# Token halves of the MLP made the halves of the output projection: the first half turned between its last products, four first products over 512 tokens among the second half's norms

## The chip, the cores and the metric

The kernel runs on one core of one Trainium2 chip. The metric is the device time of one execution in microseconds (us), the median over several runs; lower is better. The engines are named as the profile names them: PE (TensorE matmuls), PEld (TensorE weight loads), DVE (VectorE), ACT (ScalarE), POOL (GpSimd) and SP (SyncE, which issues most DMAs).

## What is computed

One residual block over 1024 tokens of 1024 channels in float32: two parallel mixers on a normalised input, a gated merge, then the part that the change touches, an output projection, a second RMS norm, an MLP with a squared ReLU, and a final norm. Cut to that part, the reference is:

```python
h = x.astype(jnp.float32) + merged @ w_out[layer].astype(f32)

hn = rmsnorm(h, norm2_g[layer])
a = jnp.square(jax.nn.relu(hn @ w_ff1[layer].astype(f32)))
h = h + a @ w_ff2[layer].astype(f32)
...
return rmsnorm(h, final_g).astype(x.dtype)
```

with SEQ = 1024, D_MODEL = 1024 and D_FF = 4096, and `rmsnorm(x, g)` = x · rsqrt(mean(x²) + 1e-6) · g for each token.

## The kernel before, in words

**Precision.** Each float32 operand of a large product is split into a high part (a cast to fp32r on ACT, line 142, tiles that end in `h`) and a low part (the difference, a subtraction on DVE, line 147, tiles that end in `l`). A product of two split operands is three matmuls: high by high, high by low, low by high (`three`, line 490, recorded by line 121). A product of this stage has four steps of 128 in its contraction, so it is 12 matmuls of 128x512.

**Seven products in place of eight.** The output projection and both MLP products are done by a scheme of the Strassen-Winograd kind: each matrix is cut into two by two blocks, and seven products of sums of blocks replace eight. For the first MLP product the token side is cut into two halves (q = 0 and 1) and the channels into two. The class `Quads` (line 282) holds the token side. `raw[q, kp]` (tiles `hnq`) are the turned norms, channels on the partitions: kp 0 and 1 are the first half of the channels, kp 2 and 3 the second, two blocks of 128 channels to a tile. `hl[i, kp]` (tiles `sqh`, `sql`) are the split operands of product i. Products 1 and 2 use the raw first token half; 6, 5, 7 and 3 use sums of blocks (`sums`, line 341; tiles `sq1` and `hnq` again), and 4 uses a raw block of the second token half.

**The stage.** The stage of the change goes from the last products of the output projection to the first of the MLP (lines 2036 to 2104):

- The output projection ends with `pwV` products for token blocks 4 to 7 (`out_rest`, four of them) and `pwZ` products for the same blocks (`out_last`). A token block is 128 tokens. Its residual rows are in `hres[tb]` (tile `h`); blocks 0 to 3 are one half of the projection's tokens, 4 to 7 the other. Each `pwV` and `pwZ` product is added to `hres[4]` to `hres[7]` by DVE (line 1072). Blocks 0 to 3 are final before the `pwV` products begin; block 4+n is final only after the n-th `pwZ` product.
- Each finished block is normalised (`norm2_token`, line 1443): ACT squares it with a sum (line 1451; block 7 in two pieces, added on POOL by line 1458), POOL scales and takes the power -0.5 (lines 230 and 233), DVE multiplies (line 1462, tile `hn`), and POOL issues the DMA that stores the block (line 1467).
- The norms are turned (`Quads.fill`, line 304): 16 transposes of 128x128 on PE (line 124, into banks `hnt`), four to a bank, then ACT copies the bank to `hnq` (line 329). The first token half is split at once.
- In this kernel the MLP's token halves are the even and the odd token blocks. So every pair of blocks, one even, one odd, gives 128 tokens to each half: the first pair (0, 1) is turned as soon as it is normalised, and the half-done operands let products 1 and 2 of the first two column blocks (`w1`, `w2`; bank `pW`) run over 256 tokens at a time (matmuls of 128x256) as the pairs come in.
- Then come products 6 (`x6`, bank `pX`), 5 (`y5`, bank `pY`), 7, 4 and 3 of the two column blocks, and after them the loop over the other column blocks (`mlp_up`). Product 6 needs the sums of both token halves, and the sums of weights `t1h`, `t1l`.

**What sets the order.** Each engine runs its instructions in the order in which the program gives them to it. The order is that of the calls in the main part, changed by a scheduler under ordering hints: `after(...)` puts one instruction behind another on an engine without a semaphore; ACT copies and squares are chained by `last_evac`; the `sums` and `sum_lo` of DVE are put behind the last low part (`last_lo`). PE is strictly in order within the "fill" lane, where all products of this stage are.

**The end of the kernel.** The second MLP product lands its seven products in `hres` (`land`, line 1901), and `finish_tokens` (line 1809) takes the final norm of each block: the even blocks in the last group's first four steps, the odd ones at the very end.

Of the kernel before, what the change touches and what calls it, by code (L numbers as in the profile page):

```python
# [14 lines left out]
ALU = mybir.AluOpType  # L15
# [4 lines left out]
P = 128  # L20
T = 1024
D = 1024
NT = T // P
KT = D // P
# [15 lines left out]
def kernel(  # L40
# [19 lines left out]
    nc = tc.nc  # L60
# [14 lines left out]
    def slot(name, dt=F32):  # L75
        return spool.tile([P, 1024], dt, tag="s", name=name)
# [216 lines left out]
    class Quads:  # L293
# [7 lines left out]
        def part(t, pr, n):  # L301
            return t.rearrange("p (k t) -> p k t", k=2)[:, :, pr * P : (pr + n) * P]

        def fill(self, pr, src, name):


            banks = []
            for kp in range(KT // 2):
                if pr == 0:
                    for q in range(2):  # L310
                        self.raw[q, kp] = slot(f"{name}q{q}{kp}")
                pb = bank(f"{name}t{pr}{kp}")
                open_block("fill")
                for q in range(2):
# [12 lines left out]
        def leave(self, pr, q, kp, pb):  # L327
            last_evac[0] = after(
                nc.scalar.copy(
                    self.part(self.raw[q, kp], pr, 1),  # L330
                    pb[:, q * 256 : (q + 1) * 256].rearrange("p (k t) -> p k t", k=2),
                ),
                last_evac[0],
            )
# [7 lines left out]
        def sums(self, pr, n, first=True, then=True):  # L342
            r = self.raw

            def tt(out, a, b, op):
                after(
                    nc.vector.tensor_tensor(
                        out=self.part(out, pr, n),
                        in0=self.part(a, pr, n),
                        in1=self.part(b, pr, n),  # L350
                        op=op,
                    ),
                    self.last_lo,
                )

            for kp in range(2):
                if pr == 0 and first:
                    self.s1.append(slot(f"sq1{kp}"))
                if first:
                    tt(self.s1[kp], r[1, kp], r[1, kp + 2], ALU.add)  # L360
                    tt(r[1, kp], r[0, kp], r[1, kp], ALU.subtract)
                    tt(r[0, kp], self.s1[kp], r[0, kp], ALU.subtract)
            for kp in range(2):
                if then:
                    tt(r[0, kp + 2], r[0, kp + 2], r[0, kp], ALU.subtract)

        def sum_form(self, i):
# [8 lines left out]
            for kp in range(2):  # L376
                self.split(i, kp, src[kp])

        def form(self, i, k, c0=0, n=512):
            h, l = self.hl[i, k // 2]  # L380
            c = (k % 2) * 512 + c0
            return h[:, c : c + n], l[:, c : c + n]


    class Unit:
# [1205 lines left out]
    class UpPair:  # L1591
# [63 lines left out]
            self.sum_hi(i)  # L1655
            self.sum_lo(i)

        def product(self, i, ps, start, stop=False, c0=0, n=512, ks=range(4)):
            open_block("fill")
            wh, wl = self.w[i]  # L1660
            for k in ks:
                xh, xl = hn.form(i, k, c0, n)
                three(
                    ps[:, c0 : c0 + n], wh[:, k], wl[:, k], xh, xl, start and k == 0, k == 3, True
                )

        def put(self, m, t, n=1):
            dst = ad[self.j // 2][:, m - 1 : m - 1 + n, self.j % 2, :]
# [2 lines left out]

        def w1(self, c0=0, n=512):
            if c0 == 0:
                self.W = bank(f"pW{self.j}")
                self.p1 = half(f"p1_{self.j}")
            self.product(1, self.W, True, False, c0, n)
            last_evac[0] = nc.scalar.copy(self.p1[:, c0 : c0 + n], self.W[:, c0 : c0 + n])

        def w2(self, c0=0, n=512, ks=range(4)):
            self.product(2, self.W, False, True, c0, n, ks)
            if c0 + n == 512:
                self.a11 = half(f"a11_{self.j}")
                relu_square(self.a11, self.W)
                self.put(3, self.a11)

        def x6(self):
            self.X = bank(f"pX{self.j}")
# [210 lines left out]

    def land(m, tb):
        for q, sign in LANDS[m]:
            h = hres[2 * tb + int(q[0]) - 1]
            cs = slice((int(q[1]) - 1) * 512, int(q[1]) * 512)
            ins = (add if sign > 0 else sub)(h[:, cs], h[:, cs], pmb[m, tb])
        return ins

    def mlp_down():
        for i, (gi, c) in enumerate(steps):
# [5 lines left out]
            if not last or c < NCH - 2:  # L1915
                for o in ops[i]:
                    for tb in range(4):
                        down_products(c, tb, *o)
                        if c == NCH - 1:
                            land(o[0], tb)  # L1920
            else:
                for tb in range(4):
                    for b in (1, 0):
                        down_products(c - b, tb, *ops[i - b][0])
                    landed = land(6, tb)
                    half_ssq(2 * tb + 1, 1)
                    if tb:
                        finish_tokens(2 * tb - 1, landed)
                finish_tokens(NT - 1)
            if i < NT - 1:  # L1930
                for tb in (0, 1) if i == 0 else (i + 1,):
# [3 lines left out]
                gfb[0] = slot("gf")  # L1935
                load(gfb[0], final_g.partition_broadcast(P))
            if last and c < 4:
                half_ssq(2 * c, 0)
                half_ssq(2 * c, 1)
                finish_tokens(2 * c)  # L1940
                half_ssq(2 * c + 1, 0)
                mul(hres[2 * c + 1][:, 0:512], hres[2 * c + 1][:, 0:512], gfb[0][:, 0:512])


    for tb in (0, 1):
# [146 lines left out]
    first[0].sum_split(0)  # L2092
    hn.sum_form(5)
    first[1].sum_hi(0)
    after(first[1].sum_lo(0), hn.last_lo)
    for u in first:
        u.y5()
    hn.sum_form(7)
    for u in first:
        u.x7()  # L2100
    hn.sums(2, 2, first=False)
    hn.sum_form(4)
    pairs[2].split()
    pairs[2].sums()
# [38 lines left out]
```

## Time and profile before

| what | value |
|---|---|
| median of 3 runs | 1470.97 us (1469.83 to 1471.96) |
| span of the profiled execution | 1469.2 us, 20065 instructions |
| busy in the span: PE, PEld | 1441.4 us (98%), 1227.8 us (84%) |
| busy in the span: DVE, ACT, POOL | 1105.7 us (75%), 671.9 us (46%), 132.0 us (9%) |
| mean granted TensorE clock | 0.993 |
| the stage of the change | about 809 to 863 us of the span |

The span goes from the first to the last instruction of one profiled execution; no time of that execution apart from its span is given, and the median of the unprofiled runs lies 1.8 us above the span. Rows of the timeline show the start, the duration, the engine, the line of the code, the operation, output<-inputs and their shape, the number of merged instructions, and in square brackets how long the engine was idle before and who ended that. Matmuls overlap, so the distance between two starts, not the duration, is what one costs. A wait on PE is only lost time if nothing else could be on PE, and as PE is in order, it always is.

### The profile page before, as it was taken

The numbers are of one execution on the slowest core, as the hardware profiler recorded it, in microseconds if no ns is written. First come the engines' busy times: TensorE is split into PE (matmuls) and PEld (weight loads), VectorE is DVE, ScalarE is ACT, GpSimd is POOL, SyncE is SP. The second block draws the span as 40 slices with busy tenths as digits, with TensorE's granted clock in tenths as the row PEclk, the third lists the DMA queues.
The fourth block names the chain that finished last, engine by engine and source line by source line (L and its number), as shares of the span: only waits on it lengthen the run. The fifth ranks groups of instructions, "written<-read, shape, count | busy, mean of one in ns | idle before, by whom it ended". The sixth has DMA issues, their size and how long they took to land.

```text
span 1469.2 us, 20065 instructions
## 1 busy us (share of the span) xinstructions
PE 1441.4 (98%) x7490; PEld 1227.8 (84%) x7490; DVE 1105.7 (75%) x1591; ACT 671.9 (46%) x1180; POOL 132.0 (9%) x319
## 2 busy tenths in 40 slices
PE   8999998999999999999999899999999999999997
PEld 8889987988898888888888688888888888888886
DVE  6699797789657788877777888666766666768765
ACT  7566665552313234532344465444444533533433
POOL 3121111000000002100010300000000000000032
PEclk9999999999999999999999999999999999999999
DMA  7144255001313148665589223444444975676834
GB/s 206 35 119 101 46 106 110 27 15 44 93 30 100 51 129 234 227 208 179 170 270 302 101 79 123 158 158 158 157 157 158 345 272 201 231 276 246 281 104 179
DMA packets 157736, 227.30 MB, mean 155 GB/s; under 512 B 25308, under 2 KB 92936, under 8 KB 157640
## 3 DMA queue, kind: packets, MB, share of 16 engines
q1 hardware_dynamic: 142664, 184.07, 37.3%
q0 software_dynamic: 11376, 35.40, 9.3%
q10 hardware_dynamic: 3600, 6.56, 1.2%
q8 instruction: 59, 0.97, 0.3%
q14 instruction: 37, 0.30, 0.1%
HBM read 163.34 MB, written 62.65 MB: 154 GB/s over the span
## 4 chain that ended last, share of the span: by engine, by line
PE 89%; DVE 5%; DMA 2%; POOL 1%; issue 1%; ACT 1%; SPq 0%; POOLq 0%; ACTq 0%; DVEq 0%
PE pm L121 18%; PE pX L121 9%; PE pjqk L121 6%; PE pY L121 6%; PE pW L121 6%; PE pjv L121 3%; PE pys L121 3%; PE gY L121 3%; PE gX L121 3%; PE pyh L121 3%; PE pji L121 3%; PE pjg L121 3%; PE pjf L121 3%; PE po L121 3%; PE pjq L121 2%; PE z L121 2%
## 5 line engine op out<-in xcount | busy, mean ns | idle before, releaser
L142 ACT CAST whid<-w 128x1024 fp32r<-128x1024 f32 x31 | 32.6, 1052 | 154.1 <-PE pm L121 86.2
L679 DVE TENSOR_TENSOR_SCAN rm<-rm,bits 128x511 f32<-128x511 f32 (+7 forms) x72 | 87.3, 1219 | 15.2 <-ACT rm L657 13.5
L121 PE MATMUL pm<-wlod,sh 128*128 128x512 f32 x248 | 96.7, 390 | 0.7 <-DVE wlod L147 0.7
L121 PE MATMUL pm<-whid,sl 128*128 128x512 f32 x248 | 96.6, 390 | 0.0
L121 PE MATMUL pm<-whid,sh 128*128 128x512 f32 x248 | 96.6, 389 | 0.0
L147 DVE TENSOR_TENSOR wlod<-w,whid 128x1024 fp32r<-128x1024 f32 x31 | 37.9, 1223 | 57.2 <-ACT whid L142 57.2
L121 PE MATMUL pm<-th,sh 128*128 128x512 f32 x200 | 77.9, 390 | 0.0
L121 PE MATMUL pm<-th,sl 128*128 128x512 f32 x200 | 77.9, 389 | 0.0
L121 PE MATMUL pm<-tl,sh 128*128 128x512 f32 x200 | 77.9, 389 | 0.0
L147 DVE TENSOR_TENSOR sl<-sa,sh 128x1024 fp32r<-128x1024 f32 x56 | 68.3, 1219 | 0.8 <-ACT sh L142 0.8
L142 ACT CAST wTh<-pw 128x512 fp32r<-128x512 f32 (+3 forms) x96 | 44.4, 488 | 46.0 <-PE pw L124 40.4
L142 ACT CAST sh<-sa 128x1024 fp32r<-128x1024 f32 x56 | 57.2, 1046 | 10.9 <-DMA sa<-ad 10.9
L147 DVE TENSOR_TENSOR wTl<-pw,wTh 128x512 fp32r<-128x512 f32 (+3 forms) x96 | 50.8, 548 | 10.1 <-ACT wTh L142 5.6
L121 PEld LDWEIGHTS pm<-wlod,sh 128*128 128x128 f32 x248 | 46.6, 188 | 10.8 <-DVE wlod L147 1.1
L1809 POOL TENSOR_SCALAR fss<-fss 128x1 f32<-128x1 f32 x8 | 4.5, 561 | 563.0 <-ACT fsc L1804 562.5
L121 PEld LDWEIGHTS pm<-whid,sh 128*128 128x128 f32 x248 | 46.6, 188 | 9.6
L121 PEld LDWEIGHTS pm<-whid,sl 128*128 128x128 f32 x248 | 46.5, 188 | 9.6
L155 DVE TENSOR_TENSOR bt<-bt,rm 128x511 f32<-128x511 f32 (+7 forms) x72 | 48.9, 687 | 5.0 <-ACT wf0h L142 0.5
L657 ACT ACTIVATE rm<-z 128x511 f32<-128x511 f32 (+6 forms) x96 | 47.5, 502 | 5.8 <-DVE bt L155 2.6
L121 PE MATMUL pX<-sqh,t1h 128*128 128x512 f32 x128 | 49.9, 390 | 0.0
L121 PE MATMUL pX<-sql,t1h 128*128 128x512 f32 x128 | 49.9, 390 | 0.0
L121 PE MATMUL pX<-sqh,t1l 128*128 128x512 f32 x128 | 49.8, 389 | 0.0
(920 smaller groups left out, 4613.7 us busy)
## 6 DMA issues: line engine op xcount, KB each, us to landing
w<-in_w_ff_dram SPq DMA_DIRECT2D x72, 512.0 KB, 5.0
sa<-ad SPq DMA_DIRECT2D x56, 512.0 KB, 6.4
ad<-a SPq DMA_DIRECT2D x32, 256.0 KB, 4.2
ad<-s SPq DMA_DIRECT2D x16, 512.0 KB, 3.4
tw<-in_w_out_dram POOLq DMA_DIRECT2D x6, 1024.0 KB, 7.6
x<-in_x_dram SPq DMA_DIRECT2D x8, 512.0 KB, 9.4
xnl<-xnh POOLq DMA_DIRECT2D x8, 512.0 KB, 11.9
pr<-pd SPq DMA_DIRECT2D x8, 512.0 KB, 6.5
```

What stands on the lines that cost most here:

```text
L121: return pe(nc.tensor.matmul(*a, **k))
L142: in_turn("act", nc.scalar.copy(dst, src))
L147: nc.vector.tensor_tensor(out=dst, in0=src, in1=hi.bitcast(F32), op=ALU.subtract),
L155: return nc.vector.tensor_tensor(out=out, in0=a, in1=b, op=ALU.mult)
L657: nc.scalar.activation(rm[:, s0 + c0 - 1 : s0 + m - 1], z[:, c0:m], AF.Sigmoid, scale=-0.125)
L679: sc = nc.vector.tensor_tensor_scan(out=rr, data0=rr, data1=bits[:, 1024 - nk + a : 1024 - nk + b][:, ::-1], initial=rm[:, b : b + 1] if i ...
L1809: nc.gpsimd.tensor_scalar(out=ssq, in0=ssq, scalar1=1.0 / D, scalar2=EPS, op0=ALU.mult, op1=ALU.add)
```

## The change

The MLP's token halves become blocks 0 to 3 and blocks 4 to 7, the halves that the output projection already has. Since blocks 0 to 3 are final first, the first half is turned early: pair (0, 1) behind the second `pwV` product and pair (2, 3) behind the fourth. The second half is turned after all `pwZ` products: pair (4, 5) behind the first column block's `w1`, pair (6, 7) behind its `w2` and the second's `w1`. The four products `w1` and `w2` of the two column blocks run once over 512 tokens, where before they ran twice over 256. The sums of the second half come in two calls of `sums` for each kp. `sum_lo(1)` of both column blocks now stands behind all of product 6's token operands, where before the first one's stood between the early products. The load of the third pair of weights moves from behind the last norm to behind block 5's. `land` and the order of `finish_tokens` follow the new numbering.

```diff
-        def fill(self, pr, src, name):
-            banks = []
-            for kp in range(KT // 2):
...
-                for q in range(2):
-                    for j in range(2):
-                        kt, b = 2 * kp + j, 2 * q + j
-                        transpose(
-                            pb[:, b * P : (b + 1) * P],
-                            src[2 * pr + q][:, kt * P : (kt + 1) * P],
-                        )
-                banks.append(pb)
-                self.leave(pr, 0, kp, pb)
-                self.split(1 + kp // 2, kp % 2, self.raw[0, kp], pr, 1)
-            for kp in range(KT // 2):
-                self.leave(pr, 1, kp, banks[kp])
+        def fill(self, q, pr, src, name):
+            b0 = 2 * pr
+            banks = {}
+            order = (0, 2, 1, 3) if q else range(4)
+            for kp in order:
...
+                for j in range(2):
+                    for i in range(2):
+                        kt, b = 2 * kp + j, 2 * j + i
+                        transpose(
+                            pb[:, b * P : (b + 1) * P],
+                            src[4 * q + b0 + i][:, kt * P : (kt + 1) * P],
+                        )
+                self.leave(q, b0, kp, pb)
+                if q == 0:
+                    self.split(1 + kp // 2, kp % 2, self.raw[0, kp], b0, 2)
...
+        def sums(self, pr, n, kp):
             r = self.raw
+            if pr == 0:
+                self.s1.append(slot(f"sq1{kp}"))
+            self.tt(pr, n, self.s1[kp], r[1, kp], r[1, kp + 2], ALU.add)
+            self.tt(pr, n, r[1, kp], r[0, kp], r[1, kp], ALU.subtract)
+            self.tt(pr, n, r[0, kp], self.s1[kp], r[0, kp], ALU.subtract)
...
-            if tb % 2 == 1 and n == 0:
+            if tb >= 4 and n == 0:
                 nc.scalar.mul(y[:, cs], hres[tb][:, cs], r)
...
-            q = nc.gpsimd if tb % 2 == 0 else nc.scalar if tb == NT - 1 and n == 0 else nc.sync
+            q = nc.gpsimd if tb < 4 else nc.scalar if tb == NT - 1 and n == 0 else nc.sync
...
-            h = hres[2 * tb + int(q[0]) - 1]
+            h = hres[4 * (int(q[0]) - 1) + tb]
...
-        if tb > 1:
-            hn.fill(tb - 2, hsrc, "hn")
-        if tb == 3:
-            hn.sums(0, 1)
+        if tb in (1, 3):
+            hn.fill(0, tb // 2, hsrc, "hn")
     for tb in range(4, NT):
         out_last(tb - 4)
         if tb == NT - 1:
             for u in first:
                 last_evac[0] = after(u.sum_hi(1), last_evac[0])
-            first[0].w1(0, 256)
+            first[0].w1()
         side = norm2_token(tb)
-        next(side)
-        if tb == NT - 1:
-            hn.sums(2, 1, then=False)
-        if tb == 6:
-            hn.fill(2, hsrc, "hn")
         for _ in side:
             pass
-    pairs[2].load()
-    first[1].w1(0, 256)
-    first[0].w2(0, 256)
-    first[0].sum_lo(1)
-    first[1].w2(0, 256, range(2))
-    hn.sums(1, 1)
-    hn.fill(3, hsrc, "hn")
-    first[1].w2(0, 256, range(2, 4))
-    for u in first:
-        u.w1(256, 256)
-    for u in first:
-        u.w2(256, 256)
-    hn.sums(3, 1, then=False)
-    hn.sum_form(6)
-    after(first[1].sum_lo(1), hn.last_lo)
+        if tb == 5:
+            pairs[2].load()
+    hn.fill(1, 0, hsrc, "hn")
+    for kp in range(2):
+        hn.sums(0, 2, kp)
+    first[0].w2()
+    first[1].w1()
+    hn.fill(1, 1, hsrc, "hn")
+    first[1].w2()
+    for kp in range(2):
+        hn.sums(2, 2, kp)
+        hn.sum_form(6, (kp,))
+    for u in first:
+        after(u.sum_lo(1), hn.last_lo)
     for u in first:
         u.x6()
```

On PE, around the second `pwV` product (`pwV5`, token block 5): `hn0` and `hn1` are the norms of blocks 0 and 1, `hnt` the banks that their transposes fill. Before:

```order
L121 MATMUL pwV5_7991<-wout21h1_7733,mbl1_7805 128x512
L121 MATMUL pwV6_8009<-wout21h0_7729,mbh0_7798 128x512
...
L121 MATMUL pwV6_8009<-wout21h1_7733,mbl1_7805 128x512
L124 MATMUL hnt00_8025<-ident_73,hn0_7880 128x128 x2
L124 MATMUL hnt00_8025<-ident_73,hn1_7901 128x128 x2
...
L121 MATMUL pwV7_8075<-wout21h0_7729,mbh0_7798 128x512
```

With the change:

```order
L121 MATMUL pwV5_7991<-wout21h1_7733,mbl1_7805 128x512
L124 MATMUL hnt000_8010<-ident_73,hn0_7880 128x128
L124 MATMUL hnt000_8010<-ident_73,hn1_7901 128x128
...
L124 MATMUL hnt003_8043<-ident_73,hn1_7901 128x128
L121 MATMUL pwV6_8053<-wout21h0_7729,mbh0_7798 128x512
```

The 16 transposes of the first pair have moved ahead of the third `pwV` product, and the two blocks alternate from one transpose to the next.

On DVE, ahead of the first product 6 (`pX0`): `sq10`, `sq11`, `hnq00`, `hnq01`, `hnq10` and `hnq11` are the sums of the token blocks, `sql60` and `sql61` the low parts of product 6's token operand for kp 0 and 1, and `t1l0` and `t1l1` the low parts of its weights for the two column blocks. Before (`t1l0` stands 18 rows further up, ahead of the norm of block 7):

```order
L347 TENSOR_TENSOR sq10_8125<-hnq10_8024,hnq12_8048 128x2x128
L347 TENSOR_TENSOR sq11_8129<-hnq11_8036,hnq13_8060 128x2x128
L347 TENSOR_TENSOR hnq10_8024<-hnq00_8023,hnq10_8024 128x2x128
L347 TENSOR_TENSOR hnq11_8036<-hnq01_8035,hnq11_8036 128x2x128
L347 TENSOR_TENSOR hnq00_8023<-sq10_8125,hnq00_8023 128x2x128
L347 TENSOR_TENSOR hnq01_8035<-sq11_8129,hnq01_8035 128x2x128
L147 TENSOR_TENSOR sql60_8447<-hnq00_8023,sqh60_8446 128x1024
L147 TENSOR_TENSOR sql61_8451<-hnq01_8035,sqh61_8450 128x1024
L147 TENSOR_TENSOR t1l1_8258<-w1_1r1_7769,t1h1_8257 128x1024
```

With the change:

```order
L342 TENSOR_TENSOR hnq01_8020<-sq11_8266,hnq01_8020 128x2x256
L342 TENSOR_TENSOR sq10_8262<-hnq10_8234,hnq12_8241 128x2x256
L342 TENSOR_TENSOR hnq10_8234<-hnq00_8009,hnq10_8234 128x2x256
L342 TENSOR_TENSOR hnq00_8009<-sq10_8262,hnq00_8009 128x2x256
L147 TENSOR_TENSOR sql60_8345<-hnq00_8009,sqh60_8344 128x1024
L342 TENSOR_TENSOR sq11_8266<-hnq11_8248,hnq13_8255 128x2x256
L342 TENSOR_TENSOR hnq11_8248<-hnq01_8020,hnq11_8248 128x2x256
L342 TENSOR_TENSOR hnq01_8020<-sq11_8266,hnq01_8020 128x2x256
L147 TENSOR_TENSOR sql61_8352<-hnq01_8020,sqh61_8351 128x1024
L147 TENSOR_TENSOR t1l0_8201<-w1_0r1_7752,t1h0_8200 128x1024
L147 TENSOR_TENSOR t1l1_8204<-w1_1r1_7769,t1h1_8203 128x1024
```

The three sums of kp 0 are followed by their low part, then the three of kp 1 by theirs, and `t1l0`, which product 6 reads in its third matmul, has moved from ahead of block 7's norm to behind all of them. Of the row at the top, six such sums over the first 256 tokens stand ahead, directly behind block 7's norm.

On PE, between the last transposes and the first product 6, before:

```order
L124 MATMUL hnt33_8364<-ident_73,hn7_8275 128x128 x2
L121 MATMUL pW1_8298<-sqh21_8067,whiu1_7859 128x256
...
L121 MATMUL pW0_8260<-sqh10_8031,b11h0_7834 128x256
...
L121 MATMUL pW1_8298<-sqh21_8067,wlou1_7860 128x256
L121 MATMUL pX0_8455<-sqh60_8446,t1h0_8254 128x512
```

With the change:

```order
L121 MATMUL pW1_8286<-sqh21_8049,whiu1_7859 128x512
...
L121 MATMUL pW1_8286<-sqh21_8049,wlou1_7860 128x512
L121 MATMUL pX0_8357<-sqh60_8344,t1h0_8200 128x512
L121 MATMUL pX0_8357<-sql60_8345,t1h0_8200 128x512
L121 MATMUL pX0_8357<-sqh60_8344,t1l0_8201 128x512
```

Before, 54 matmuls of 256 columns stand between the last transpose and product 6; now there are 12 of 512 columns, one `w2`.

More of the change, by code (lines that the diff above doesn't have):

```diff
@@ L340, in split, with tt, last_sum, sum_form @@
             self.last_lo = hi_lo(h, l, self.part(src, pr, n))
-        def sums(self, pr, n, first=True, then=True):
-            r = self.raw
[L345 to L353, printed above, removed]
-                )
[L356 to L367, printed above, removed]
+        def tt(self, pr, n, out, a, b, op):
+            after(
+                nc.vector.tensor_tensor(
+                    out=self.part(out, pr, n),
+                    in0=self.part(a, pr, n),
+                    in1=self.part(b, pr, n),
+                    op=op,
+                ),
+                self.last_lo,
+            )
+        def sums(self, pr, n, kp):
+            r = self.raw
+            if pr == 0:
[3 more added lines that the diff above has]
+            self.tt(pr, n, r[0, kp], self.s1[kp], r[0, kp], ALU.subtract)
+        def last_sum(self, kp):
+            r = self.raw
+            self.tt(0, 4, r[0, kp + 2], r[0, kp + 2], r[0, kp], ALU.subtract)
+        def sum_form(self, i, kps=range(2)):
             r = self.raw
@@ L375, in sum_form, with form @@
             }[i]
-            for kp in range(2):
+            for kp in kps:
                 self.split(i, kp, src[kp])
-        def form(self, i, k, c0=0, n=512):
+        def form(self, i, k):
             h, l = self.hl[i, k // 2]
-            c = (k % 2) * 512 + c0
-            return h[:, c : c + n], l[:, c : c + n]
+            c = (k % 2) * 512
+            return h[:, c : c + 512], l[:, c : c + 512]
     class Unit:
@@ L1656, in sum_split, with product @@
             self.sum_lo(i)
-        def product(self, i, ps, start, stop=False, c0=0, n=512, ks=range(4)):
+        def product(self, i, ps, start, stop=False):
             open_block("fill")
             wh, wl = self.w[i]
[L1661 to L1665, printed above, removed]
+            for k in range(4):
+                xh, xl = hn.form(i, k)
+                three(ps, wh[:, k], wl[:, k], xh, xl, start and k == 0, k == 3, True)
         def put(self, m, t, n=1):
@@ L1669, in put, with w1, w2 @@
             nc.sync.dma_start(dst, t.rearrange("p (m t) -> p m t", m=n))
[L1674 to L1686, printed above, removed]
+        def w1(self):
+            self.W = bank(f"pW{self.j}")
+            self.p1 = half(f"p1_{self.j}")
+            self.product(1, self.W, True)
+            last_evac[0] = nc.scalar.copy(self.p1, self.W)
+        def w2(self):
+            self.product(2, self.W, False, True)
+            self.a11 = half(f"a11_{self.j}")
+            relu_square(self.a11, self.W)
+            self.put(3, self.a11)
         def x6(self):
@@ L2100 @@
         u.x7()
-    hn.sums(2, 2, first=False)
+    for kp in range(2):
+        hn.last_sum(kp)
     hn.sum_form(4)
```

30 lines of the change are left out of this document (14 added, 16 removed).

## The prediction

> **What bounds the kernel now.** I read the page first, for the engine that sets the end.
>
> ```profile
> PE 1441.4 (98%) x7490; PEld 1227.8 (84%) x7490; DVE 1105.7 (75%) x1591; ACT 671.9 (46%) x1180; POOL 132.0 (9%) x319
> PE 89%; DVE 5%; DMA 2%; POOL 1%; issue 1%; ACT 1%; SPq 0%; POOLq 0%; ACTq 0%; DVEq 0%
> ```
>
> PE is busy for 98% and makes up 89% of the chain that ended last. So only two things move the time: PE's own work, and the places where PE waits. Next I read PE's timeline through the stage, of which these are the rows where something other than an evenly spaced matmul happens, and the starts of the groups behind them.
>
> ```profile
> 819.84 0.44 PE L124 MATMUL hnt<-ident,hn 128*128 128x128 f32 x2 [0.59 <-DVE hn L1462]
> 821.04 1.75 PE L124 MATMUL hnt<-ident,hn 128*128 128x128 f32 x14 [0.76 <-DVE hn L1462]
> 822.54 0.48 PE L121 MATMUL pwV<-wout21h,mbh 128*128 128x512 f32 x1
> 825.37 2.26 PE L124 MATMUL hnt<-ident,hn 128*128 128x128 f32 x16
> 827.38 0.48 PE L121 MATMUL pwZ<-wout22h,m4h 128*128 128x512 f32 x1
> 838.44 0.41 PE L124 MATMUL hnt<-ident,hn 128*128 128x128 f32 x2 [2.62 <-DVE hn L1462]
> 840.35 3.25 PE L124 MATMUL hnt<-ident,hn 128*128 128x128 f32 x14 [1.50 <-DVE hn L1462]
> 843.25 0.77 PE L121 MATMUL pwZ<-wout22h,m4h 128*128 128x512 f32 x1
> 847.20 0.28 PE L121 MATMUL pW<-sqh,b11h 128*128 128x256 f32 x1
> 852.22 0.38 PE L124 MATMUL hnt<-ident,hn 128*128 128x128 f32 x2
> 854.39 1.75 PE L124 MATMUL hnt<-ident,hn 128*128 128x128 f32 x14 [1.79 <-DVE hn L1462]
> 855.89 0.37 PE L121 MATMUL pW<-sqh,whiu 128*128 128x256 f32 x1
> 862.46 0.40 PE L121 MATMUL pX<-sqh,t1h 128*128 128x512 f32 x1
> ```
>
> Three of the four turnings wait for a norm (idle 0.59 and 0.76, 2.62 and 1.50, 1.79); the second (825.37 to 827.38) does not, and shows that 16 transposes cost 2.01 us when nothing is late. The chain of waits and the busy time by stretch give the price of a product and what follows.
>
> ```profile
> 755.05 10.88 PE pwW L121 x48
> 856.14 6.49 PE pW L121 x54
> ```
>
> ```profile
> 862.40:889.70 27.30, 27.30 (x123) 1.00 0.10 39
> ```
>
> 48 matmuls of 512 columns take 10.88 us, so a product of 12 takes 2.72; 54 of 256 columns take 6.49, so one takes 0.12 and a 512-column pair in two pieces 0.24, against 0.227 in one. From the first `pX` on, PE is busy through all of 27.30 us. So what reaches the first `pX` late is late at the end.
>
> The last view is the granted clock around the long waits (the column with 1.00 or 0.50 before the last two).
>
> ```profile
> 251.00:255.10 4.10, 0.00 (x0) 0.00 (x0) 0.93 (x1) 2.00 (x4) 0.00 (x0) 1.00 0.53 142
> 255.10:258.50 3.40, 2.44 (x11) 2.44 (x12) 3.40 (x6) 2.04 (x8) 0.38 (x3) 0.50 0.50 151
> 258.50:261.90 3.40, 3.40 (x11) 2.92 (x11) 3.26 (x8) 2.18 (x6) 0.00 (x0) 0.50 0.01 3
> 838.40:840.30 1.90, 0.41 (x2) 0.20 (x2) 1.29 (x2) 0.00 (x0) 0.55 (x1) 0.60 0.00 0
> 840.30:843.20 2.90, 2.85 (x14) 2.85 (x15) 0.97 (x2) 2.13 (x6) 1.13 (x3) 0.50 0.54 152
> 843.20:845.60 2.40, 2.40 (x8) 1.91 (x7) 1.94 (x5) 2.40 (x10) 0.47 (x1) 0.50 1.02 322
> 845.60:848.00 2.40, 2.40 (x15) 2.08 (x14) 0.99 (x3) 1.91 (x3) 0.00 (x0) 1.00 0.96 288
> 852.00:854.40 2.40, 0.61 (x7) 0.38 (x5) 1.40 (x3) 0.00 (x0) 1.37 (x3) 1.00 0.05 17
> ```
>
> After the wait near 251 and after the pair 2.62 and 1.50 the clock is at 0.50 until 261.9 and 845.6; after 1.79 it stays at 1.00. Such a spell costs half of the busy time in it: 840.35 to 845.6 is 5.25, so 2.6 us; in the other, 2.44 + 3.40 busy cost 2.9.
>
> **What the change takes away.** I count from 827.38, where the `pwZ` products begin, to 862.46.
> - The third turning goes from between the `pwZ` products, where it takes 843.25 − (835.43 + 0.23) = 7.6 us with its waits, to behind `w1`. By then PE has one more `pwZ` and a `w1` in front, 5.4 us, against a wait of 2.6 + 1.5. It should cost 2.0: gain 5.6. (835.43 is the start of the last matmul ahead of it.)
>
> ```profile
> 835.43 0.39 PE L121 MATMUL pwZ<-wout22h,m4l 128*128 128x512 f32 x1
> ```
>
> - The clock spell's rest on the last `pwZ`: 847.20 − 843.25 = 3.95 against 2.72: gain 1.2.
> - The fourth turning, 855.89 − 852.22 = 3.7 against 2.0: gain 1.7, if block 7's norm is in time (below).
> - 96 matmuls of 256 columns at 0.12 become 48 at 0.227: 11.5 − 10.9, gain 0.6.
>
> Together 9.1. The smaller edits cost nothing on PE: the copies and low parts of the first half are fewer and larger, and stand beside the `pwZ` products; the load of the third weights goes out earlier on SP; POOL's store of block 7 now goes ahead of block 6's power, but waits only for a `pwZ` that is long done; the tail has the same count of finishes in the same places. I take 0 for these, with ±0.3.
>
> **What it adds, first: 2.7 us.** The first turning needs block 1's norm at 821.04, set by DVE:
>
> ```profile
> 818.51 4.87 DVE L1462 SCALAR_TENSOR_TENSOR hn<-h,n_y,g2b 128x1024 f32<-128x1024 f32 x4
> ```
>
> These four stand behind the addition of the second `pwV` and the same weight sums in both orders, so the turning ends at 822.5 as before. But the third `pwV` product, which covered 2.72 of the wait, now comes behind it. `pwZ` begins 2.7 later, at 830.1, and PE is idle from about 816.6 to 821.0 but for a transpose at 819.8.
>
> **What it adds, second: a wait at product 6.** From 830.1 PE runs four `pwZ` (10.9), `w1` (2.7), a turning (2.0), `w2` and `w1` (5.4): the last turning begins at T = 851.15. Only one `w2` stands between it and product 6, whose third matmul would be due at T + 2.0 + 2.7 + 0.45 = T + 5.2. It reads `t1l0`, the last of a chain between ACT and DVE. Its steps come from these rows: the copy of 512 columns from a bank, the cast, the low part, the sum of 512 elements (two in 1.29, so 0.60 apart and 0.69 to the end), `t1l`.
>
> ```profile
> L1679 ACT COPY p<-pW x18: 359/567/588, 848.8 to 1134.7; 128x512 f32<-128x512 f32 x14, 128x256 f32<-128x256 f32 x4
> ```
>
> ```profile
> 860.06 2.00 ACT L142 CAST sqh<-hnq 128x1024 fp32r<-128x1024 f32 x2
> ```
>
> ```profile
> 861.14 2.36 DVE L147 TENSOR_TENSOR sql<-hnq,sqh 128x1024 fp32r<-128x1024 f32 x2 [0.78 <-ACT sqh L142]
> 863.42 1.22 DVE L147 TENSOR_TENSOR t1l<-w_1r,t1h 128x1024 fp32r<-128x1024 f32 x1
> 872.68 1.29 DVE L347 TENSOR_TENSOR hnq<-hnq,hnq 128x512 f32<-128x512 f32 x2
> ```
>
> 1. Banks of kp 0 and 2 copied, behind `w1`'s copy, three ACT copies at 0.5 to 0.57: T + 1.9.
> 2. Three sums of kp 0, each waiting for the one before (0.69 + 0.05): 2.2. Cast 1.05, low part 1.22, two handovers of 0.07: 2.4. Together 4.6.
> 3. The same for kp 1, which DVE starts only behind kp 0's low part, less an overlap of 0.1: 4.5.
> 4. `t1l0`: 1.15.
>
> So T + 12.2, 7.0 behind its due time; PE is idle but for two matmuls. In the old order the same steps stood beside 54 quarter-width matmuls (6.5 us), and `t1l0` was made before.
>
> Is anything later still? Block 7's norm is: `w1` ends at 843.7, its copy precedes the squares on ACT. These rows are that path before.
>
> ```profile
> 848.82 0.37 ACT L1679 COPY p<-pW 128x256 f32<-128x256 f32 x1 [1.31 <-PE pW L121]
> ```
>
> ```profile
> 850.51 2.11 POOL L1458 TENSOR_TENSOR n_ss<-n_ss,n_ss 128x1 f32<-128x1 f32 x1 [1.52 <-ACT hn L1451]
> 852.99 0.56 POOL L233 TENSOR_TENSOR n_y<-n_ss,expo 128x1 f32<-128x1 f32 x1
> ```
>
> ```profile
> 851.36 1.22 DVE L147 TENSOR_TENSOR t1l<-w_0r,t1h 128x1024 fp32r<-128x1024 f32 x1
> 853.58 1.41 DVE L1462 SCALAR_TENSOR_TENSOR hn<-h,n_y,g2b 128x512 f32<-128x512 f32 x2 [1.00 <-POOL n_y L233]
> ```
>
> From the copy to the norm: 854.99 − 848.82 = 6.2. The wider copy adds 0.2. POOL's addition took 2.11, where the power takes 0.56; all that time DVE ran without a gap, until `t1l` ended at 852.58, and now DVE has nothing between block 6's norm and block 7's. I take 0.56 for it, the nearest row of the kind, and keep 2.11 as its other end. So 843.9 + 4.9 = 848.8, in time for the turning at 851.15; six sums of the first 256 tokens at 0.6 follow, to 852.4, ahead of T + 1.9 = 853.05. With 2.11 they end at 854.0, 0.9 later. The Trainium skill (SBUF — State Buffer, "SBUF: two separate sides") says that a VectorE instruction with two SBUF inputs and a GpSimd one lock each other out for a whole instruction. The trace agrees: the 2.11 us ended with DVE's last subtraction of that run; by this rule the addition is short now, and by its absence the sum would be 0.9 higher.
>
> **What it adds, third: the clock.** The first new wait, 3.2 and 0.8 us around one transpose, is longer than the 2.62 and 1.50 that halved the clock; the second, 7.0 us with two matmuls, much longer. PE is the bound behind both, so each spell costs what the rows above show, 2.6 (to 2.9; never more than half of 6.8 us, the whole length of each spell, 3.4): together 5.2.
>
> **Sum:** −9.1 + 2.7 + 7.0 + 5.2 = **+5.8 us**. The span of the profiled execution goes from 1469.2 to 1475.0; the median lies 1.8 above the span, so 1470.97 + 5.8 = **1476.8 us**.
>
> **The rivals.**
> - *The first wait leaves the clock alone.* For it: 1.79 us did not lower the clock, and the transposes at 819.8 break the wait up. Against it: two did not help at 838.4, in a shorter wait. It gives +0.6 + 2.6 = +3.2, 1474.2. The Trainium skill (TensorE: Matmul & The Clock Gate, "What's actually happening") lets the clock fall only after an idle window of about 3.4 us, counted freely. By that rule neither piece of the first wait would do; the trace of the spell at 838.8 disagrees, since its longest idle piece was 2.62.
> - *Neither wait lowers the clock:* +0.6, 1471.6, no change. Only a second wait far below 7 us would do that; 4.1 us without a matmul did lower it near 251.
> - *The other side: the gains win, since product 6 hardly waits.* In the old order the chain from the last turning to the second low part of product 6 (854.39 to 863.5, 9.1 us) never stopped PE. If kp 1's sums ran beside kp 0's cast and `t1l0` ahead, up to all 7.0 and a spell of 2.6 vanish: 5.8 − 9.6 = −3.8, 1467.2. It decides at about T + 6.4: ready before that, the kernel isn't slower. Against it: DVE's order puts each in a row, and the copies and kp 0's steps alone end at T + 6.5.
> - *Dearer:* POOL's addition at 2.11 (+0.9) and both spells at their full 3.4 (+1.6): +8.3, 1479.3.
>
> **How the numbers follow.** Chances: forecast 0.50, first wait without a spell 0.22, no spell 0.08, other side 0.06, dearer 0.14. A measurement can tell about 0.2%, 2.9 us, from no change. Slower by more than that: forecast, dearer, and a bit over half of the second case (+3.2 with ±1.1, the spread of the three runs): 0.77. Within: the rest of that case and the third: 0.17. Faster: 0.06. The range covers the second case, the forecast and the dearer end, with 1.0 to 1.5 around them: 1472.7 to 1480.3.
>
> **What would show it.** In the changed profile: the first transposes at about 819.8 and 821.0 with 3 us idle ahead and `pwZ` at 830 or, after a spell, 832 to 833; no wait ahead of the two second-half turnings; in the third matmul of `pX` an idle time of 5 us or more put down to DVE `t1l`, 12 us behind the last turning's start; the granted clock at 0.50 around 822 and around 866; no wait from there to `pW` of the third column block. It is wrong if PE waits for a norm in the second half (block 5's or 7's path is longer), if `pX` runs through, or if a new wait shows behind it.

## The result, and the profile after

The changed kernel takes **1474.9 us** (median of 8 runs, 1473.11 to 1477.42) against 1470.68 for the kernel before, run beside it (1469.4 to 1471.96): ratio 1.0029, 95% interval 1.0019 to 1.0039. It is slower, by 4.2 us (0.3%) where 5.8 were forecast. Its profiled execution took 1474.41 us with a span of 1472.3.

The page answers to the two lines of before: PE is still busy for 98% and now makes up 92% of the chain, so what counts is PE's waits and PE's speed.

```profile
PE 1442.0 (98%) x7442; PEld 1225.6 (83%) x7442; DVE 1105.0 (75%) x1567; ACT 670.6 (46%) x1154; POOL 129.8 (9%) x319
...
PE 92%; DVE 3%; DMA 1%; issue 1%; ACT 1%; POOL 1%; SPq 0%; POOLq 0%; DVEq 0%; ACTq 0%
```

PE's timeline through the stage, those rows where something other than an evenly spaced matmul happens. Start, duration, engine, line, operation, output<-inputs, shape, count; in brackets the idle time ahead and who ended it.

```profile
819.35 0.33 PE L124 MATMUL hnt<-ident,hn 128*128 128x128 f32 x1 [3.31 <-DVE hn L1458]
820.55 2.90 PE L124 MATMUL hnt<-ident,hn 128*128 128x128 f32 x15 [0.87 <-DVE hn L1458]
...
829.36 1.91 PE L124 MATMUL hnt<-ident,hn 128*128 128x128 f32 x16
831.02 0.48 PE L121 MATMUL pwZ<-wout22h,m4h 128*128 128x512 f32 x1
...
844.72 1.91 PE L124 MATMUL hnt<-ident,hn 128*128 128x128 f32 x16
...
851.93 1.91 PE L124 MATMUL hnt<-ident,hn 128*128 128x128 f32 x16
853.59 0.48 PE L121 MATMUL pW<-sqh,whiu 128*128 128x512 f32 x1
857.00 0.50 PE L121 MATMUL pX<-sqh,t1h 128*128 128x512 f32 x1 [0.43 <-ACT sqh L142]
858.26 0.49 PE L121 MATMUL pX<-sql,t1h 128*128 128x512 f32 x1 [0.76 <-DVE sql L147]
863.79 0.79 PE L121 MATMUL pX<-sqh,t1l 128*128 128x512 f32 x1 [5.03 <-DVE t1l L147]
871.33 0.39 PE L121 MATMUL pY<-sqh,t0h 128*128 128x512 f32 x1
```

The three waits of before (for the first, third and fourth turning) have become two: one of 3.31 and 0.87 ahead of the first turning, and one of 0.43, 0.76 and 5.03 at product 6. The three turnings behind it do not wait at all. Next, the busy time of each engine in stretches of 3.41 us around the two waits (length, PE, PEld, DVE, ACT, POOL, then the granted clock).

```profile
817.76:821.17 3.41, 0.95 (x7) 0.77 (x8) 3.41 (x4) 0.00 (x0) 0.02 (x1) 1.00 0.00 0
821.17:824.59 3.42, 3.42 (x16) 3.13 (x15) 3.42 (x4) 3.31 (x6) 0.00 (x0) 0.50 0.02 5
...
858.72:862.13 3.41, 0.04 (x1) 0.00 (x0) 2.23 (x4) 1.83 (x2) 0.00 (x0) 1.00 0.20 79
862.13:865.55 3.42, 1.76 (x4) 1.47 (x5) 3.42 (x4) 3.42 (x5) 0.00 (x0) 0.50 0.00 0
865.55:868.96 3.41, 3.41 (x9) 2.64 (x9) 3.23 (x4) 2.19 (x3) 0.00 (x0) 0.50 0.00 0
868.96:893.09 24.13, 24.13 (x107) 19.91 (x107) 20.24 (x25) 11.78 (x17) 0.00 (x0) 1.00 0.06 22
```

The clock is halved behind each wait, from 821.17 to 824.59 and from 862.13 to 868.96, and from 868.96 to the third column block PE has no gap. Last, DVE's timeline, which says why product 6 waits.

```profile
853.72 0.69 DVE L342 TENSOR_TENSOR sq<-hnq,hnq 128x512 f32<-128x512 f32 x1 [0.74 <-ACT hnq L327]
...
856.98 1.23 DVE L147 TENSOR_TENSOR sql<-hnq,sqh 128x1024 fp32r<-128x1024 f32 x1 [1.11 <-ACT sqh L142]
858.12 0.68 DVE L342 TENSOR_TENSOR sq<-hnq,hnq 128x512 f32<-128x512 f32 x1
...
861.37 1.23 DVE L147 TENSOR_TENSOR sql<-hnq,sqh 128x1024 fp32r<-128x1024 f32 x1 [1.11 <-ACT sqh L142]
862.51 1.22 DVE L147 TENSOR_TENSOR t1l<-w_0r,t1h 128x1024 fp32r<-128x1024 f32 x1
```

Sums, a cast's wait of 1.11, a low part, the same again for kp 1, and then `t1l`: one row, in DVE's order. `t1l` ends at 863.73 and the third matmul of `pX` starts at 863.79.

**One measure for all kernels.** Each profiled execution has its own offset from earlier work (the changed kernel's is 0.49 us less than that of before), so I count the stage from the `pwV` matmul that waits for `mbl` (1.30 us in every trace) to the first `pW` of the third column block. The ratio of the times, last column, is independent of it. All values are in us.

| kernel | `mbl` matmul | first `pwZ` | third block's `pW` | stage | against before | median | ratio (95% interval) |
|---|---|---|---|---|---|---|---|
| before | 812.57 | 827.38 | 889.69 | 77.12 | | | |
| changed | 812.08 | 831.02 | 893.09 | 81.01 | +3.9 | 1474.9 | 1.0029 (1.0019 to 1.0039) |
| 1: late first turning | 813.31 | 828.07 | 890.68 | 77.37 | +0.2 | 1471.04 | 1.0011 (1.0002 to 1.0019) |
| 2: `t1l` early | 812.49 | 831.20 | 891.30 | 78.81 | +1.7 | 1472.41 | 1.0020 (1.0010 to 1.0031) |
| 3: 2 and sums first | 815.69 | 835.51 | 892.52 | 76.83 | −0.3 | 1468.89 | 0.9997 (0.9988 to 1.0005) |
| 4: 1 and 3 | 811.71 | 826.50 | 884.39 | 72.68 | −4.4 | 1466.27 | 0.9973 (0.9962 to 0.9983) |
| 5: PE busy before product 6 | 811.76 | 831.22 | 890.88 | 79.12 | +2.0 | 1472.30 | 1.0013 (1.0004 to 1.0022) |
| 6: PE busy before first turning | 811.49 | 828.75 | 891.17 | 79.68 | +2.6 | 1472.58 | 1.0016 (1.0007 to 1.0025) |
| 7: 4 and `w1` later | 811.02 | 825.78 | 882.91 | 71.89 | −5.2 | 1466.74 | 0.9974 (0.9963 to 0.9984) |
| 8: 4 and PE busy | 812.58 | 827.35 | 883.53 | 70.95 | −6.2 | 1464.53 | 0.9960 (0.9947 to 0.9972) |

The kernel before took 1470.39 in the runs beside 1 to 4 and 1469.89 beside 5 to 8, so kernels of different groups are best compared by the ratio. It lies near the ratio of the means, and so differs from that of the two medians by up to 0.0007 (experiments 1 and 3). Each stage comes from one execution.

### The profile page after: what moved, and what is told of

Read it like the earlier page. It is cut to its first block, busy times and chain, and to the rows that moved or that the text cites. A ratio compares the mean times of both kernels' runs of the same rounds, so it can differ in the third digit from the quotient of the medians.

```text
span 1472.3 us, 19913 instructions
## 1 busy us (share of the span) xinstructions
PE 1442.0 (98%) x7442; PEld 1225.6 (83%) x7442; DVE 1105.0 (75%) x1567; ACT 670.6 (46%) x1154; POOL 129.8 (9%) x319
## 4 chain that ended last, share of the span: by engine, by line
PE 92%; DVE 3%; DMA 1%; issue 1%; ACT 1%; POOL 1%; SPq 0%; POOLq 0%; DVEq 0%; ACTq 0%
PE pm L121 18%; PE pX L121 9%; PE pjqk L121 6%; PE pY L121 6%; PE pW L121 6%; PE pjv L121 3%; PE pga L121 3%; PE pys L121 3%; PE gY L121 3%; PE gX L121 3%; PE pyh L121 3%; PE pji L121 3%; PE pjg L121 3%; PE pjf L121 3%; PE po L121 3%; PE pjq L121 2%
```

## The experiments

The theory is that of the prediction: the change loses by two new waits of PE and by the clock that falls behind each, and what it gains is real. The rivals were that the clock costs nothing, and that the lost third `pwV` or `t1l` is not what product 6 or the first turning waits for.

**1: the first turning put back where it was late.** Pair (0, 1) behind the third `pwV`, pair (2, 3) behind the fourth; all else as in the changed kernel.

```diff
-        if tb in (1, 3):
-            hn.fill(0, tb // 2, hsrc, "hn")
+        if tb > 1:
+            hn.fill(0, tb - 2, hsrc, "hn")
```

> The first pair of blocks is turned behind the third output product again and the second behind the fourth; all else is as changed. Theory (two new waits, each with a clock spell): the product that covered 2.7 us of the wait is back in front, the wait is 1.4 us as before and the clock stays at 1.00 there, so the last output products begin 4.1 to 4.4 us earlier and the time falls from 1474.9 to about 1470.6, with the wait at product 6 unchanged at 6 to 7 us. Rival (the wait at product 6 takes up whatever comes earlier, since it is set by VectorE): 1474.9, the wait at product 6 grows by 4 us.

Measured: 1471.04. PE's timeline there:

```profile
820.54 0.33 PE L124 MATMUL hnt<-ident,hn 128*128 128x128 f32 x1 [0.59 <-DVE hn L1458]
821.74 1.86 PE L124 MATMUL hnt<-ident,hn 128*128 128x128 f32 x15 [0.87 <-DVE hn L1458]
...
828.07 0.48 PE L121 MATMUL pwZ<-wout22h,m4h 128*128 128x512 f32 x1
...
861.16 0.80 PE L121 MATMUL pX<-sqh,t1l 128*128 128x512 f32 x1 [5.02 <-DVE t1l L147]
```

The third `pwV` covers the wait again (0.59 in place of 3.31), the 15 transposes take 1.86 in place of 2.90, and `pwZ` begins 14.76 behind the `mbl` matmul, as before (14.81), not 18.94. Product 6's wait stays, with a longer clock spell (10.2 us, 856.56 to 866.80). So the early first turning costs about 4 us (3.6 in the stage, 4.2 at the first `pwZ`).

**2: `t1l` ahead of block 7's norm on DVE**, for both column blocks.

```diff
         side = norm2_token(tb)
+        next(side)
+        if tb == NT - 1:
+            for u in first:
+                u.sum_lo(1)
...
-    for u in first:
-        after(u.sum_lo(1), hn.last_lo)
```

> Only the low parts of the weight sums for product 6 are moved ahead of block 7's norm on VectorE, where it idles for about 1.8 us. Theory (product 6 waits for the last link of a chain, these low parts): its third matmul runs at once, the wait moves to its eighth, which reads the low part of the second half of the channels, made 1.1 us before; gain 1.1 + 5 x 0.23 = 2.3 us, and up to 2.6 more if the clock stays up: 1470.0 to 1472.6. Rival (block 7's norm or the sums ahead bind, so that putting work ahead of them delays them): no gain or a loss of 2.3 us, 1474.9 to 1477.2.

Measured: 1472.41. PE's timeline at product 6:

```profile
859.12 0.40 PE L121 MATMUL pX<-sqh,t1l 128*128 128x512 f32 x1
...
861.90 0.79 PE L121 MATMUL pX<-sqh,t1h 128*128 128x512 f32 x1 [1.69 <-ACT sqh L142]
863.17 0.79 PE L121 MATMUL pX<-sql,t1h 128*128 128x512 f32 x1 [0.47 <-DVE sql L147]
```

The wait for `t1l` is gone (the third matmul, at 859.12, follows the second without idle time); what shows behind it is kp 1's operands, late because kp 1's sums stand behind kp 0's low part. With the waits ahead of the first two matmuls (0.77 and 0.76), 3.7 us of idle time are left of the changed kernel's 6.2 at product 6.

**3: as 2, and all sums ahead of both splits.**

```diff
     for kp in range(2):
         hn.sums(2, 2, kp)
-        hn.sum_form(6, (kp,))
+    hn.sum_form(6)
```

> As e2, and both groups of sums run on VectorE ahead of the two low parts, so that ScalarE casts the first group while VectorE sums the second. Theory: the chain from the last turning shortens from 11.9 us to about 8.8 at the eighth matmul of product 6, the wait there falls from 6.8 to about 2.5 in pieces of 2 us, the clock stays at 1.00: 4.4 + 2.6 = 7.0 us less, 1467.9 (1470.5 if the clock falls all the same). Rival (the length of the wait does not matter, the lost cover of quarter products does): 1470 or more.

Measured: 1468.89. PE's timeline at product 6, of an execution that reached the stage 2.4 to 4.7 us later than those of the other kernels and was the slowest of its twelve runs (1474.59):

```profile
862.31 0.50 PE L121 MATMUL pX<-sqh,t1h 128*128 128x512 f32 x1 [1.25 <-ACT sqh L142]
863.70 0.79 PE L121 MATMUL pX<-sql,t1h 128*128 128x512 f32 x1 [0.88 <-DVE sql L147]
```

kp 1's sums now fill DVE's 1.11 us beside kp 0's cast, the third matmul follows at once, and 2.1 us of idle time are left. Experiments 2 and 3 leave the amount of DVE's work as it is, so its order was 4.1 of the 6.2. The clock still falls (863.61 to 867.03).

**4: 1 and 3 together.**

> e1 and e3 together. Theory: the two waits are separate, so the gains add: 4.3 + 7.0 = 11.3 less than 1474.9, 1463.6 (1466.2 if the clock falls at product 6), faster than the kernel before by 0.3 to 0.5 per cent. Rival (the waits are one, since both end in the same VectorE chain): the gains overlap and it is no better than the better of the two, about 1468.

Measured: 1466.27, 0.9973 of before: faster than both kernels. The two repairs add up (−3.6 and −4.2 in the stage make −8.3). PE's timeline at product 6, the only wait of the second half that is left:

```profile
854.18 0.50 PE L121 MATMUL pX<-sqh,t1h 128*128 128x512 f32 x1 [2.13 <-ACT sqh L142]
855.56 0.50 PE L121 MATMUL pX<-sql,t1h 128*128 128x512 f32 x1 [0.88 <-DVE sql L147]
```

**5: PE kept busy ahead of product 6.** Experiments 5, 6 and 8 put extra matmuls (fillers) into PE's waits; what they compute is thrown away.

```diff
+            if self.j == 0:
+                open_block("fill")
+                for _ in range(26):
+                    matmul(self.X, pairs[1].w[2][0][:, 0], hn.form(2, 0)[0], start=True, stop=True)
```

> The changed kernel, with 26 more matmuls of 128x512 put on PE right ahead of product 6 (26 x 0.227 = 5.9 us). They write the bank that product 6 then starts anew, so what they compute is thrown away. They stand in the time in which PE waits anyway (0.43 + 0.76 + 5.03 = 6.2 us), so product 6's third matmul is still released by t1l, at the same time. What they change is the granted clock: PE is no longer idle. Theory (the second spell, 862.13 to 868.96, costs half of the 5.2 us of work in it): no spell there, 2.6 us less than the changed kernel, 1472.3 us. Rival (the clock in that spell costs nothing that counts, only the wait does): no difference, 1474.9 us; if the added matmuls delay product 6, later than that.

Measured: 1472.30. PE's timeline and the granted clock there:

```profile
856.62 6.06 PE L121 MATMUL pX<-sqh,whiu 128*128 128x512 f32 x26
...
864.00 0.50 PE L121 MATMUL pX<-sqh,t1l 128*128 128x512 f32 x1 [0.88 <-DVE t1l L147]
```

```profile
858.91:862.33 3.42, 3.42 (x17) 2.83 (x16) 2.24 (x4) 1.83 (x2) 0.00 (x0) 1.00 0.21 79
```

`t1l` still releases the third matmul, so the wait is the same; the clock stays at 1.00 and the stage is 1.9 shorter, though the first spell fell out longer in this execution (6.8 us, `pwZ` 0.5 later). The second spell costs 2.4.

**6: PE kept busy ahead of the first turning.**

```diff
+                if q == 0 and pr == 0 and kp == 0:
+                    for _ in range(16):
+                        matmul(
+                            pb, merged["b"][0][0][:, 0:P], out_form["21"].hl[0][0][:, 0:512],
+                            start=True, stop=True,
+                        )
```

> The changed kernel, with 16 more matmuls of 128x512 (3.6 us) put on PE ahead of the first turning, into the bank that the turning's transposes then overwrite; what they compute is thrown away. They stand in the wait of 3.31 us for block 0's norm. Theory: the spell of the clock at 821.17 to 824.59 goes, and with it the half of the work that stood in it, 1.4 to 1.7 us: 1473.2 to 1473.5 us; the wait for block 1's norm stays. Rival (the first spell costs nothing, the turning and the products catch up before product 6, which waits for ACT and DVE): t1l is late by the same amount either way only if its chain starts with PE; if the chain's start does not move, 1474.9 us.

Measured: 1472.58, below the 1473.2 to 1473.5 of the theory; the kernel before was 0.8 faster in these runs than in those beside the changed kernel. PE's timeline:

```profile
815.25 3.80 PE L121 MATMUL hnt<-wout21h,mbh 128*128 128x512 f32 x16
...
819.91 1.86 PE L124 MATMUL hnt<-ident,hn 128*128 128x128 f32 x15 [0.76 <-DVE hn L1464]
```

No spell at the first turning (1.86 for 15 transposes), and `pwZ` begins 17.26 behind the `mbl` matmul in place of 18.94: the first spell costs 1.7. Of that the stage keeps 1.3, because the second spell was longer in this execution (10.2 us, 857.22 to 867.46). The rival falls: the chain behind product 6 starts with PE.

**7: the fourth experiment with one more product behind the last turning.**

```diff
-    first[1].w1()
     hn.fill(1, 1, hsrc, "hn")
+    first[1].w1()
```

> The fourth experiment's kernel (late first turning, sums first), with the second column block's w1 moved behind the last turning, so that two products instead of one stand between the last turning and product 6. Theory A (product 6's wait is only as long as too little of PE's work stands behind the last turning): 2.7 us more work covers the waits of 2.13 and 0.88 us and their spell (1.7): up to 4.7 us less, 1461.6 us. Theory B (the turning cannot go 2.7 us earlier, since block 7's norm is ready only 7.4 us after the last pwZ product ends, and the six sums on DVE stand in front of it): PE waits ahead of the turning instead, and the time stays within 0.8 of the fourth experiment's 1466.3 us.

Measured: 1466.74, the same as 4 within either interval. PE's timeline:

```profile
845.57 2.08 PE L124 MATMUL hnt<-ident,hn 128*128 128x128 f32 x15 [1.33 <-DVE hn L1458]
...
851.10 0.50 PE L121 MATMUL pW<-sqh,whiu 128*128 128x512 f32 x1 [0.68 <-ACT p L1672]
...
855.20 0.50 PE L121 MATMUL pX<-sql,t1h 128*128 128x512 f32 x1 [0.77 <-DVE sql L147]
```

Theory B holds: the wait moves to block 7's norm and to the chain of sums, and the time stays where it was. The clock does not fall in this execution's stage, so the spell that cost 1.7 in 4 is gone, but the stage is only 0.8 shorter: the waits have grown by about 0.9. What bounds the stage now is that chain from the last `pwZ` product through norm, copies, sums and split.

**8: the fourth experiment with 9 fillers.**

> The fourth experiment's kernel (late first turning, sums first), with 9 more matmuls of 128x512 (2.0 us) ahead of product 6, in the bank that product 6 starts anew; what they compute is thrown away. They stand in its waits of 2.13 and 0.88 us. Theory: the spell of the clock at 856.44 to 859.85 goes, half of 3.4 us, 1.7 us less than the fourth experiment: 1464.6 us. Rival (two matmuls in the wait and 2 us of fillers leave the clock as it is, or the spell costs nothing): 1466.3 us.

Measured: 1464.53, 0.9960 of before, the fastest of all. PE's timeline:

```profile
852.74 2.20 PE L121 MATMUL pX<-sqh,whiu 128*128 128x512 f32 x9
...
856.41 0.50 PE L121 MATMUL pX<-sql,t1h 128*128 128x512 f32 x1 [0.87 <-DVE sql L147]
```

The clock never falls in this stage, and the stage is 1.7 shorter than in 4: half of the 3.4 us of the spell. The intervals of 4 and 8 overlap, but the traces name the difference.

## Why the prediction was right, and where its sizes were off

The direction, the two places, the releasing instructions and the two spells came as forecast; the sum was +5.8, the stage shows +3.9, the medians +4.2. Term by term:

- **Gains, −9.1 forecast, −9.7 measured.** From the first `pwZ` to the point where product 6 could start, 35.08 us before; now 856.41 − 831.02 = 25.4 (856.41 is where the last matmul of `w2` has been issued). The turnings were mis-sized: I took 2.01 for 16 transposes that wait for nothing. They take 853.59 − 851.93 = 1.66 (and 831.02 − 829.36 = 1.66), so 0.7 more is gained on two. The merged row of before hid a gap, which the same timeline shows when it is cut there:

```profile
825.37 1.47 PE L124 MATMUL hnt<-ident,hn 128*128 128x128 f32 x12
...
826.97 0.66 PE L124 MATMUL hnt<-ident,hn 128*128 128x128 f32 x4
```

Twelve transposes start 0.109 apart, 825.37 to 826.56; the thirteenth only at 826.97, 0.4 later. A row without brackets is not a row without a wait, since the brackets show only the idle time ahead of its first instruction.

- **The late first turning, +2.7 forecast.** `pwZ` begins 4.1 later than before (18.94 − 14.81). Of that, 2.7 is the `pwV` product that no longer covers the wait, 1.7 the clock, and −0.35 the second turning, which has lost the gap above. Experiment 1 takes back all of it, experiment 6 the clock's part.
- **The first spell, +2.6 forecast, 1.7 measured.** It lasted 3.4 us, not the 6.8 of the two spells of before. The forecast's weak step was to take a spell's length for a constant; the last section shows what sets it. How far off it was is partly luck: experiments 3 and 5 leave the first turning as it is, their spell there lasted 6.8, and `pwZ` began 0.9 and 0.5 later than in the changed kernel's trace. The rival that the first wait leaves the clock alone (0.22) is refuted by the window from 821.17.
- **The wait at product 6, +7.0 forecast, 6.9 measured** (863.79 against 856.41 + 0.45). The chain came to T + 11.9 for T + 12.2, and the turning was 0.34 shorter; the two cancel. Experiments 2 and 3 show which of its steps can be moved: `t1l`, and kp 1's sums behind kp 0's low part.
- **The second spell, +2.6 forecast.** 871.33 − 863.79 = 7.54 for 22 matmuls that need 22 x 0.227 = 4.99: 2.5. Experiment 5 takes away 2.4.
- **Block 7's norm** is in time. POOL's addition took 0.19, below my 0.56 and far from the 2.11 of before. Experiment 2 shows the cover that I had named: there `t1l` runs on DVE at 846.24 to 848.59, and POOL's scalar steps of the same norm, 128x1 each, are drawn out to 0.51 and 1.04. POOL's timelines, the changed kernel and then experiment 2:

```profile
846.82 0.19 POOL L1454 TENSOR_TENSOR n_ss<-n_ss,n_ss 128x1 f32<-128x1 f32 x1 [2.00 <-ACT hn L1447]
847.10 0.19 POOL L230 TENSOR_SCALAR n_ss<-n_ss 128x1 f32<-128x1 f32 x1
```

```profile
847.00 0.51 POOL L1454 TENSOR_TENSOR n_ss<-n_ss,n_ss 128x1 f32<-128x1 f32 x1 [2.00 <-ACT hn L1447]
847.59 1.04 POOL L230 TENSOR_SCALAR n_ss<-n_ss 128x1 f32<-128x1 f32 x1
```

The two steps end at 847.51 and 848.63, just behind the ends of the two `t1l` (847.46 and 848.59). The Trainium skill (SBUF — State Buffer, "SBUF: two separate sides") lets one of the two, a VectorE instruction with two SBUF inputs or a GpSimd one that reads SBUF, hold their shared port for a whole instruction while the other waits; these rows agree.

- **The other side** (0.06) needed kp 1's sums beside kp 0's cast and `t1l` ahead. In this kernel neither happens, as DVE's order said; experiment 3 makes both happen and comes to 1468.89, which against the kernel before is no clear change (0.9997, interval 0.9988 to 1.0005), where this rival had −3.8. Its mechanism was right in part: the idle time at product 6 falls from 6.2 to 2.1, but what is left still lowers the clock, and the first turning's loss stays.

Added up: −9.7 + 4.1 + 6.9 + 2.5 = +3.8, against +3.9 in the stage. Of the 2.0 that the forecast had too much, 0.9 are the first spell, 0.35 the second turning and 0.6 the other two; the rest is spread over the last terms. The range, 1472.7 to 1480.3, held the time.

## What to carry to other kernels

A larger tile that starts earlier takes work away from where it covered someone's wait: ask of every product that is moved or merged what stood behind it, because here what was removed was worth 9.7 us, and the two new waits cost 9.6 before the clock was counted. When an in-order engine produces several operands for the next step, put all steps of the same kind ahead of those that wait for another engine (all sums, then all low parts), and tiles without late inputs (`t1l`) ahead of both; this and one product of cover turned +4.2 us into −4.1. Where a short wait cannot be removed, useless matmuls in it keep the clock up, which took 1.3 to 1.9 us off the stage here.

## What was not expected of the hardware

**The length of a clock spell.** In each execution all changes of the clock lie on one grid of 3.41 us: in the changed kernel 261.39, 821.17, 824.59, 862.13 and 868.96 are 164, 1, 11 and 2 steps apart. Cut by that grid, every window says what the next one gets. Beside the windows of the changed kernel above, here are three more traces, with the columns as there. Experiment 4, where a window with two waits in it is followed by one at half speed:

```profile
853.02:856.44 3.42, 1.38 (x5) 0.93 (x6) 3.31 (x5) 3.36 (x5) 0.00 (x0) 1.00 0.00 0
856.44:859.85 3.41, 3.41 (x10) 2.63 (x9) 1.60 (x2) 3.41 (x5) 0.00 (x0) 0.50 0.20 77
```

Experiment 6, where the clock falls in the middle of the wait:

```profile
853.81:857.22 3.41, 1.49 (x5) 0.44 (x3) 2.48 (x3) 1.99 (x3) 0.00 (x0) 1.00 0.15 59
857.22:860.64 3.42, 0.00 (x0) 0.00 (x0) 2.28 (x4) 2.62 (x3) 0.00 (x0) 0.50 0.05 18
860.64:864.05 3.41, 2.54 (x6) 2.06 (x7) 3.41 (x4) 3.41 (x5) 0.00 (x0) 0.50 0.00 0
```

The kernel before, where one of two windows with a wait is followed by a fall (to 0.50 from 838.78, as the prediction's rows show) and the other not:

```profile
835.37:838.78 3.41, 0.80 (x4) 0.23 (x3) 1.28 (x1) 0.93 (x2) 2.95 (x5) 1.00 0.74 308
...
852.44:855.85 3.41, 1.62 (x15) 1.46 (x14) 2.40 (x6) 0.95 (x4) 0.93 (x3) 1.00 0.02 10
```

With PE busy for 1.38 or 1.49 of 3.41 us (0.40, 0.44) the next window is at 0.50; with 1.62 (0.48) it stays at 1.00. At half speed 2.54 (0.74) keeps it there, and a full window ends it (865.55 in the changed kernel). In all ten traces, from 60 us on, no window at full speed that was busy for 0.47 or more was followed by half speed, and those with 0.44 or less were, but for one, at the end of experiment 2:

```profile
1462.25:1465.67 3.42, 1.49 (x7) 0.91 (x5) 1.51 (x3) 1.70 (x5) 1.08 (x4) 1.00 0.55 214
1465.67:1469.08 3.41, 0.00 (x0) 0.00 (x0) 0.75 (x1) 0.72 (x1) 0.55 (x1) 1.00 0.59 229
```

So PE's busy time as the profile draws it is not quite the measure. It draws 0.39 for a matmul of 512 columns whose neighbour starts 0.227 later. If each matmul counts by that distance instead (0.227 for 512 columns, 0.12 for 256, 0.109 for a transpose), the two sides part in these traces: windows up to 0.36 were followed by half speed, those from 0.39 on were not. At half speed a drawn share of 0.81 or less kept it and 0.89 or more ended it. A spell takes 3.4, 6.8 or 10.2 us by where the grid happens to fall on the wait, which the code does not set: experiments 1 and 6 had 10.2, because the clock fell in the middle of the wait. This explains the forecast's miss on the first spell, and it may be part of the spread between executions of one kernel (4.3 us for the changed one); that part was not tried by a run of its own.

The Trainium skill (TensorE: Matmul & The Clock Gate, "What's actually happening") lets the clock fall after an idle window of about 3.4 us that runs freely. The length and the free run agree with these rows (3.41); that the window must be idle does not, since one with PE busy for 1.49 us was enough. By that rule read strictly, experiment 4 would have had no spell; it had one, and experiment 8 shows its price.
